# Merged pole powers, a second mixer that ends inside attention, and a new order at the seams, in a two-layer hybrid mixer block

## The chip, the cores and the metric

The kernel runs on one core of one Trainium2 chip. The metric is the device time of one execution, in microseconds, as a median of runs. The engines are named as the profile names them: PE (TensorE, the matmuls; PEld is its weight load), DVE (VectorE), ACT (ScalarE), POOL (GpSimd) and SP (SyncE, which here issues every DMA, in program order, on one queue).

## The reference

Two layers work on 1024 latent tokens and 256 context tokens of width 1024. Each layer modulates and normalises, projects in, runs four mixers of width 256 side by side, gates them, projects out and adds to the residual.

```python
for l in range(DEPTH):                                  # 2
    need_ctx = l < DEPTH - 1
    h_l = rms_norm(x, g_pre[l]) * (1 + sc_l) + sh_l     # the same for ctx
    p_l = h_l @ w_in[l]
    a_l, a_c = mla_mixer(...)                           # attention, low-rank keys
    g_l, g_c = gqa_mixer(...)                           # attention, grouped keys
    s_l, s_c = ssm_mixer(...)                           # state-space scan, both directions
    y_l, y_c = hyena_mixer(...)                         # long convolutions by FFT
    out_l = concatenate([a_l, g_l, s_l, y_l]) @ w_out[l]
    x = x + gt_l * rms_norm(out_l, g_post[l])
    if need_ctx: ...                                    # the context only in the first layer
```

The part of the state-space mixer that moves is its discretisation (a_bar, powers of it, and b_bar, from lam, log_step and b) and its end:

```python
y = y + d_skip * u
z = gelu(y)
z = z * sigmoid(z @ glu_w + glu_b)
return z * silu(p[..., w:])
```

## The kernel before

Activations lie transposed: channels on partitions, tokens along the free dimension, in tiles of up to 512 tokens. A product in full precision is three passes over rounded halves, so that the in-projection, for instance, is a run of PE instructions ipc<-hh,whi, ipc<-hl,whi and ipc<-hh,wlo. Results that another stage needs in another layout go through DRAM: uD and yD (input and output of the scan), hyD (input of the hyena mixer), gP, gV, mK, mV, mQ, mS (keys, values and queries), gD (gates), mixD (the four mixers' outputs, 8 blocks of 128 channels).

A layer runs in this order. First the tables: the filters of the hyena mixer (`filters`, whose step by step tile is ht, and whose PE instructions are hps, brow, sps, fdft), the poles of the scan (`ssm_poles`, small DVE instructions on tiles sp and pw) and the scan's tables (`ssm_tables`, which makes sE, sF and sT on DVE and POOL, transposes sE on PE into etp, and stores all of it). In-projection blocks are woven between by the string SCRIPT. Then four lanes, in the order of the letters in LANES: s the scan (`ssm`), p the preparation of queries, keys and values (`prep`), h the long convolution (`hyena`), f the end of the scan (`ssm_finish`, with `hyena_ctx` for the context in the first layer). LANES is "spfh" in the first layer and "hspf" in the second. The lanes stand under a high priority, and the in-projection of the gates (`inproj_gate`) below it: a list scheduler takes gate matmuls where the lanes' next PE instruction is not ready in its model, so that gate matmuls are filler. What it decides is fixed in the program: each engine runs its instructions in that order, and waits where one is not ready.

The scan goes over groups of channels. For one group PE makes the drive (drv), DVE and POOL turn and scan it (sD, sV), and PE reads it out (sy, three matmuls for each of the group's channel blocks: one with smt and two with sfm). In the kernel before, sy of a group stands right behind that group's scan in the program.

Attention (`attention`) runs units of one pair of heads by 256 queries: 40 in the first layer, 32 in the second. For each it loads keys kst, values vst (once for a pair) and queries aq; makes scores aS and acx; takes row maxima am on DVE and exponentials aP on ACT; transposes apt; splits into aPh (ACT) and aPl (DVE); and makes apo. A generator `side` is pumped once or more in a unit: it makes the gate vectors, loads the output weights (owr) and, in the first layer, the modulation of the second (mraw). A list `later` holds pieces that run at the next pump. `outproj` then reads mixD (omx) and gD (ogt) tile by tile, multiplies them on DVE, splits them on ACT (omh) and POOL (oml), and makes ops on PE.

Of the kernel before, what the change touches and what calls it, by code (L numbers as in the profile page):

```python
# [187 lines left out]
class K:  # L188
# [34 lines left out]
    def mm(self, out, lhsT, rhs, start=True, stop=True):  # L223
        self.keep(self.nc.tensor.matmul(out, lhsT, rhs, start=start, stop=stop))  # L224
# [7 lines left out]
    def tt(self, out, a, b, op, eng=None):  # L232
        self.keep((eng or self.nc.vector).tensor_tensor(out=out, in0=a, in1=b, op=op))  # L233
# [17 lines left out]
    def tr(self, out, in_):  # L251
        p = in_.shape[0]
        self.keep(self.nc.tensor.transpose(out, in_, self.ident[:p, :p]))  # L253
# [52 lines left out]
    def feed(self, P, tag, shape, srcs, ahead):  # L306

        queue, srcs = [], iter(srcs)

        def more():  # L310
            src = next(srcs, None)
            if src is not None:
                t = P.tile(shape, F32, tag=tag, name=tag, bufs=ahead + 1)
                self.load(t, src)
# [8 lines left out]
    def mod_feed(self, P, blocks):  # L323

        return self.feed(P, "mraw", [128, 2, 512],
                         (self.A["w_mod"][l, b, :, k:k + 2] for l, b in blocks for k in range(0, 8, 2)), 2)
# [610 lines left out]
    def ssm_poles(self, l, P, Q):  # L937

        nc, A = self.nc, self.A
        cnt = [0]  # L940

        def t16(n=1):
            cnt[0] += 1
            return P.tile([128, 16] if n == 1 else [128, n, 16], F32, name=f"sp{cnt[0]}", tag=f"sp{cnt[0]}")
# [3 lines left out]
        self.load(lr, A["lam_re"][l])  # L948
        self.load(li, A["lam_im"][l])
        for d in range(2):  # L950
            self.load(ls[d * 64:d * 64 + 64, :], A["log_step"][l, d].partition_broadcast(64))

        def exp_parts(z):
# [11 lines left out]
            Ti = P.tile([128, 16], I32, name=f"spi{cnt[0]}", tag=f"spi{cnt[0]}")  # L965
# [44 lines left out]
        pw = P.tile([128, 2, 9, 16], F32, name="pw")  # L1010
# [8 lines left out]
        inv, qr, qi = t16(), t16(), t16()  # L1019
# [13 lines left out]
        c8 = Q.tile([128, 16], F32, name="c8")  # L1033
        ns8 = Q.tile([128, 16], F32, name="ns8")
        ts(c8, cm8, -1.0, 1.0, MUL, ADD)
        ts(ns8, s8, -1.0)
        rho = self.cp.tile([128, 16], F32, tag="rho", name="rho", bufs=2)
# [6 lines left out]
        def cm_b(o, a, b, n, eng=None):  # L1044

            u, v, w, z = (P.tile([128, 8, 16], F32, tag=f"scm{i}", name="scm")[:, :n] for i in range(4))
            br, bi = (b[i].unsqueeze(1).to_broadcast([128, n, 16]) for i in range(2))
            tt(u, a[0], br, MUL, eng)
            tt(v, a[1], bi, MUL, eng)
            tt(w, a[0], bi, MUL, eng)  # L1050
            tt(z, a[1], br, MUL, eng)
            tt(o[0], u, v, SUB, eng)
# [958 lines left out]
```

## Time and profile before

| | us |
|---|---|
| median of 3 runs | 2169.95 (2166.62 to 2171.66) |
| the profiled execution | 2168.31 |
| its span, first to last instruction | 2166.5 |
| PE busy | 1933.1 (89%) |
| DVE busy | 1557.0 (72%) |
| POOL busy | 972.2 (45%) |
| ACT busy | 896.6 (41%) |

The span is the time from the first to the last instruction, and the profiled execution's own time is 1.8 us more. Matmuls are pipelined and their busy times overlap a little. The stages of the profiled execution, in us from the span's start: start 0 to 72, first layer's tables 72 to 290, scan 295 to 417, preparation and hyena 417 to 712, attention 737 to 1058, output projection 1060 to 1210, second layer's tables to 1420, scan to 1540, the rest of its mixers to 1790, attention to 2054, output projection to the end.

### The profile page before, as it was taken

How to read it: one execution, taken by the hardware profiler on the slowest of the kernel's cores; microseconds unless marked ns; L12 is line 12 of the kernel's file. 1: busy time of each engine (PE TensorE's matmuls, PEld its weight loads, DVE VectorE, ACT ScalarE, POOL GpSimd, SP SyncE). 2: the span in 40 equal slices, each digit the busy share in tenths (PEclk: the TensorE clock that was granted, in tenths of full speed). 3: DMA queues.
4: the chain of work that ended last, by engine and by line, in shares of the span. 5: the costliest groups of instructions: out<-in, count | busy, mean ns of one | idle time of the engine just before them, and what ended most of it. 6: DMA issues, size and time to landing. Idle time of an engine off the chain costs nothing.

```text
span 2166.5 us, 31419 instructions
## 1 busy us (share of the span) xinstructions
PE 1933.1 (89%) x10811; PEld 1602.2 (74%) x10811; DVE 1557.0 (72%) x2969; ACT 896.6 (41%) x1926; POOL 972.2 (45%) x782
## 2 busy tenths in 40 slices
PE   6988998899889599899998898988889979999888
PEld 2677887777768477788777677887766667899766
DVE  5699349757776488788653498479769868999721
ACT  2422234224234367667423222344224227788611
POOL 0757236584461144434156558246566624340034
PEclk9798899899999899999899998999899989999999
DMA  7323365337656545452343423364457675561063
GB/s 254 97 91 136 108 222 142 98 118 239 201 174 197 147 126 154 139 160 80 90 142 123 139 99 130 113 232 137 128 161 223 204 213 142 150 169 46 12 184 126
DMA packets 261280, 316.55 MB, mean 146 GB/s; under 512 B 46671, under 2 KB 203599, under 8 KB 257793
## 3 DMA queue, kind: packets, MB, share of 16 engines
q1 hardware_dynamic: 261120, 314.55, 47.6%
q8 instruction: 85, 1.39, 0.3%
q14 instruction: 75, 0.61, 0.1%
HBM read 207.61 MB, written 106.86 MB: 145 GB/s over the span
## 4 chain that ended last, share of the span: by engine, by line
PE 47%; DVE 29%; DMA 10%; issue 7%; POOL 3%; ACT 2%; SPq 2%; POOLq 0%; DVEq 0%; ACTq 0%
PE ipc L224 9%; PE apo L224 7%; PE apt L253 6%; PE aS L224 6%; PE ops L224 6%; DVE lU L233 3%; DVE sD L233 3%; PE mps L224 2%; SPq L201 2%; DVE sp L233 2%; PE acx L224 2%; PE fdft L224 2%; PE hps L224 1%; DVE lX L233 1%; DVE sV L233 1%
## 5 line engine op out<-in xcount | busy, mean ns | idle before, releaser
L224 PE MATMUL ipc<-hh,whi 128*128 128x512 f32 (+2 forms) x992 | 386.7, 390 | 31.4 <-DVE ipt L236 12.8
L224 PE MATMUL ipc<-hh,wlo 128*128 128x512 f32 (+2 forms) x992 | 381.5, 385 | 3.9 <-POOL wlo L233 3.9
L224 PE MATMUL ipc<-hl,whi 128*128 128x512 f32 (+2 forms) x992 | 382.9, 386 | 0.4 <-POOL hl L233 0.4
L224 PEld LDWEIGHTS ipc<-hh,whi 128*128 128x128 f32 x992 | 196.3, 198 | 65.8 <-DVE ipt L236 15.2
L233 DVE TENSOR_TENSOR aPl<-apt,aPh 128x512 fp32r<-128x512 f32 x328 | 223.8, 683 | 20.7 <-ACT aPh L1672 16.9
L1672 ACT CAST aPh<-apt 128x512 fp32r<-128x512 f32 x328 | 186.5, 590 | 124.2 <-PE apt L253 118.3
L224 PEld LDWEIGHTS ipc<-hh,wlo 128*128 128x128 f32 x992 | 196.5, 198 | 35.2 <-POOL wlo L233 4.6
L224 PEld LDWEIGHTS ipc<-hl,whi 128*128 128x128 f32 x992 | 196.9, 198 | 31.2 <-issue 3.8
L233 POOL TENSOR_TENSOR wlo<-wraw,whi 128x512 fp32r<-128x512 f32 x92 | 139.1, 1516 | 137.1 <-ACT whi L462 103.3
L253 PE MATMUL apt<-ident,aP 128*128 128x128 f32 x1312 | 190.5, 276 | 1.2 <-DVE aPl L233 1.0
L224 PE MATMUL aS<-kst,aq 128*128 128x512 f32 x512 | 152.3, 420 | 26.4 <-DMA aq<-gP 20.8
L1637 DVE TENSOR_REDUCE am<-aS 128x1 f32<-128x1024 f32 x128 | 155.5, 1215 | 21.7 <-PE aS L224 21.6
L246 ACT ACTIVATE aP<-aS,am,rs 128x1024 f32<-128x1024 f32 x128 | 155.5, 1215 | 33.5 <-DVE am L243 32.4
L1700 POOL COPY aLB<-am 128x128 f32<-128x128 f32 x72 | 21.0, 292 | 322.8 <-DVE am L1692 322.8
L253 PEld LDWEIGHTS apt<-ident,aP 128*128 128x128 f32 x1312 | 148.3, 141 | 16.7 <-DVE aPl L233 6.4
L224 PE MATMUL apo<-aPh,vst 128*128 128x256 f32 x656 | 138.3, 308 | 15.3 <-ACT aPh L1672 8.7
L224 PE MATMUL apo<-aPl,vst 128*128 128x256 f32 x656 | 123.5, 286 | 1.6 <-DVE aPl L233 1.3
L224 PEld LDWEIGHTS aS<-kst,aq 128*128 128x128 f32 x512 | 88.2, 192 | 41.7 <-issue 21.2
L224 PEld LDWEIGHTS apo<-aPh,vst 128*128 128x128 f32 x656 | 96.2, 190 | 30.6 <-DVE aob L233 15.8
L224 PE MATMUL ops<-owh,omh 128*128 128x512 f32 x288 | 93.5, 405 | 17.1 <-ACT omh L1785 10.8
L224 PEld LDWEIGHTS apo<-aPl,vst 128*128 128x128 f32 x656 | 100.3, 189 | 8.6 <-DVE aPl L233 3.8
L224 PE MATMUL ops<-owl,omh 128*128 128x512 f32 x288 | 93.3, 404 | 0.0
(369 smaller groups left out, 4382.4 us busy)
## 6 DMA issues: line engine op xcount, KB each, us to landing
wraw<-in_w_col_dram SPq DMA_DIRECT2D x64, 256.0 KB
mraw<-in_w_mod_dram SPq DMA_DIRECT2D x32, 512.0 KB
kst<-mK SPq DMA_DIRECT2D x16, 640.0 KB
omx<-mixD SPq DMA_DIRECT2D x18, 512.0 KB
ogt<-gD SPq DMA_DIRECT2D x18, 512.0 KB
k<-kt SPq DMA_DIRECT2D x16, 512.0 KB
lk<-k SPq DMA_DIRECT2D x8, 1024.0 KB
gD<-ipt SPq DMA_DIRECT2D x32, 256.0 KB
```

Source lines behind the costliest of these rows:

```text
L201: return self.nc.sync.dma_start(out=out, in_=in_)
L224: self.keep(self.nc.tensor.matmul(out, lhsT, rhs, start=start, stop=stop))
L233: self.keep((eng or self.nc.vector).tensor_tensor(out=out, in0=a, in1=b, op=op))
L246: self.keep(self.nc.scalar.activation(out=out, in_=in_, func=func, **k))
L253: self.keep(self.nc.tensor.transpose(out, in_, self.ident[:p, :p]))
L1637: self.keep(nc.vector.tensor_reduce(out=x["m"][:, 2 + qi:3 + qi], in_=x["S"][qi], axis=AX.X, op=ALU.max))
L1672: self.keep(nc.scalar.copy(h, ps))
L1700: self.keep(nc.gpsimd.tensor_copy(x["LB"][:, :, o:o + 64], x["m"][:, 10:12].unsqueeze(2).to_broadcast([128, 2, 64])))
```

## The change

Seven things change.

1. `ssm_poles` runs once, in the first layer, for both layers: the small tiles are 128x32 instead of 128x16, the last copies (pe, pf) are made for each layer, and the second layer's result is stored in DRAM (polD) and loaded there. The products with b (bt, bb) and the loads of b and c go to a new function `ssm_drive`, called at the start of `ssm_tables`.
2. In `ssm_tables` the tile sT is made before the transposition etp, and in the first layer the first transposition of a group is put behind the last DVE instruction on sT by an added dependency (`behind`).
3. In `ssm`, the read-out sy of a group comes one group later, in the middle of the next group's scan, and in the first layer it is put behind a DVE instruction of that scan. There are three buffers for sD and two for smt.
4. LANES is "sphf" in the first layer and "hsp" in the second; the hyena mixer's buffers are freed before the last lane, and the pools of that lane lie on the other side of the memory.
5. In the second layer the end of the scan is no lane any more: `finish_steps` runs it inside attention, through `later`, in four chunks of 256 tokens, both halves of the channels in one instruction where that goes.
6. The first loads of output weights and modulation weights get an issue-order token that attention's loads also have, so they stay behind these.
7. In the second layer's output projection a pool `pad` keeps the output projection's tiles away from the place that attention's tiles held.

```diff
-LANES = "spfh", "hspf"
+LANES = "sphf", "hsp"
@@ ssm_poles
-            return P.tile([128, 16] if n == 1 else [128, n, 16], F32, name=f"sp{cnt[0]}", tag=f"sp{cnt[0]}")
+            return P.tile([128, 2, 16], F32, name=f"sp{cnt[0]}", tag=f"sp{cnt[0]}")
...
+        for l in range(2):
+            c8, ns8, _, _, pe, pf = self.pole_views(res[:, l])
+            pf0 = P.tile([128, 2, 8, 16], F32, tag="pf0", name="pf0")
+            nc.vector.tensor_copy(pe[0:64], pw[0:64, :, 7::-1, l, :])
...
+        self.polD = self.dram.tile([128, self.NPOLE], F32, name="polD")
+        self.store(self.polD, res[:, 1])
+        return res[:, 0]
+    def ssm_drive(self, l, P, qr, qi):
...
@@ dit_kernel
-                poles = k.ssm_poles(l, pt.enter_context(k.pool("polt")), Q)
+                if l == 0:
+                    poles = k.ssm_poles(pt.enter_context(k.pool("polt")), Q)
+                else:
+                    poles = Q.tile([128, k.NPOLE], F32, name="poles")
+                    k.load(poles, k.polD)
@@ ssm_tables
+            last = tt(tab[:, 0], tab[:, 0], w1, SUB)
...
             for ri in range(2):
                 ps = self.b1("etp")
                 for g in range(G):
-                    self.tr(ps[:, g * 128:g * 128 + 128], E[:, ri, g].rearrange("p t h -> p (t h)"))
+                    ins = self.tr(ps[:, g * 128:g * 128 + 128], E[:, ri, g].rearrange("p t h -> p (t h)"))
+                    if l == ri == g == 0:
+                        self.behind(ins, last)
@@ ssm
-            mt = P.tile([128, G, 128], F32, tag="smt", name="smt")
+            mt = P.tile([128, G, 128], F32, tag="smt", name="smt", bufs=2)
-            D = P.tile([128, 2, G, 160], F32, tag="sD", name="sD", bufs=2)
+            D = P.tile([128, 2, G, 160], F32, tag="sD", name="sD", bufs=3)
...
+                ins = self.mm(ps[:, g, :], mt[:, g, :], U[:, gc * G + g, lo:hi], True, False)
+                if l == g == 0 and other is not None:
+                    self.behind(ins, other)
...
-            scan(gc, *d)
+            half = scan(gc, *d)
+            other = next(half)
+            if due:
+                read(*due, other)
             yield
-            read(gc, d[1], *R)
+            for _ in half:
+                pass
             yield
+            due = gc, d[1], *R
@@ dit_kernel, the lane f
-                    with k.pool("ssf") as R:
+                    hr.close()
+                    with k.pool("ssf", side="right") as R:
                         weave(k.ssm_finish(l, R, uD, yD, need))
                         if need:
-                            with k.pool("hyc") as Q:
+                            with k.pool("hyc", side="right") as Q:
                                 weave(k.hyena_ctx(l, Q, hyD, *kf[2:]))
@@ side
                 if cols:
                     yield from k.mod_next(1, steps, M)
+                else:
+                    yield from k.finish_steps(l, M, uD, yD)
+                    for _ in range(5):
+                        yield
@@ finish_steps, for each chunk of 256 tokens, each function at a later pump
+            def skip():
+                for hf in range(2):
+                    self.stt(y[:, hf], g[:, hf], dd[:, hf:hf + 1], y[:, hf], MUL, ADD)
+                self.act(g, y, AF.Square)
+            def inner():
+                self.ts(g, g, 0.044715, 1.0, MUL, ADD)
+                self.tt(g, g, y, MUL)
+                self.act(g, g, AF.Tanh, scale=0.7978845608028654)
+            def gelu():
+                self.stt(g, g, 1.0, y, ADD, MUL)
+            def glu():
+                ps = self.f("sglu").rearrange("p (h n) -> p h n", h=2)
+                for hf in range(2):
+                    for k in range(2):
+                        self.mm(ps[:, hf], gw[:, k, hf * 128:hf * 128 + 128], g[:, k], k == 0, k == 1)
+                    self.act(y[:, hf], ps[:, hf], AF.Tanh, scale=0.25, bias=gb[:, hf:hf + 1])
+            def out():
+                self.stt(y, y, 1.0, g, ADD, MUL)
+                self.store(self.mixD[:, 4:6, c], y)
@@ feed (mod_feed and out_weights give token=self.loads, "ald0" or "ald1")
+                if token and n[0] <= ahead:
+                    self.tc.stamp_issue_order_token(ins.ins, token)
@@ output projection of the second layer
+            hp = ExitStack()
+            hp.enter_context(k.pool("pad")).tile([128, 80 * 256], F32, name="pad")
```

At the seam between the first layer's mixers and its attention, SP's queue of before holds the last mixer stores (mixD from sth and hcz; hcz is the output of the context's hyena) and the first weights of the side work ahead of the loads of keys, values and queries:

```order
L201 DMA mixD_77<-sth 128x256 x4
L201 DMA gD_78<-ipt 128x512
L201 DMA owr<-in_w_out_dram 128x512 x2
L201 DMA gD_78<-ipt 128x256
L201 DMA owr<-in_w_out_dram 128x512 x2
L201 DMA mraw<-in_w_mod_dram 128x1024 x2
L201 DMA mixD_77<-hcz_5082 128x256
L201 DMA mraw<-in_w_mod_dram 128x1024
L201 DMA mixD_77<-hcz_5090 128x256
L201 DMA kst<-gP_4000 64x2560 x2
L201 DMA vst<-gV_4001 128x10x192
L201 DMA aq<-gP_4000 64x2x256 x6
```

Of the kernel after, the same queue around the same loads:

```order
L201 DMA sgy<-yD_81 128x256
L201 DMA sgg<-uD_80 128x256
L201 DMA kst<-gP_4016 64x2560 x2
L201 DMA vst<-gV_4017 128x10x192
L201 DMA aq<-gP_4016 64x2x256 x4
L201 DMA mixD_77<-sth 128x256 x2
L201 DMA gD_78<-ipt 128x512
L201 DMA hck<-k_1313 128x1024
L201 DMA gD_78<-ipt 128x256
L201 DMA sgy<-yD_81 128x256
```

The loads for the first unit now stand ahead of the first of those stores and of the loads (hck, sgy, sgg) for the rest of lane f.

At the seam between the second layer's mixers and its attention, PE of before ends the mixers with sglu (the product with glu_w), between the first scores:

```order
L224 MATMUL ipc<-hl,whi 128x512
L224 MATMUL ipc<-hh,wlo 128x512
L224 MATMUL sglu<-sz,sgw 128x256 x4
L224 MATMUL aS<-kst,aq 128x512 x4
L224 MATMUL sglu<-sz,sgw 128x256 x4
L224 MATMUL acx<-kst,aq 128x256 x4
L224 MATMUL aS<-kst,aq 128x512 x8
```

PE of after makes one of its four sglu groups inside a unit of attention:

```order
L224 MATMUL apo<-aPh,vst 128x256 x4
L224 MATMUL apo<-aPl,vst 128x256 x4
L224 MATMUL acx<-kst,aq 128x256 x4
L224 MATMUL sglu<-sgg,sgw 128x256 x4
L262 MATMUL apt<-ident,aP 128x128 x4
L224 MATMUL apo<-aPh,vst 128x256 x2
```

What stands ahead of the first aS there is a run of 49 ipc.

At the end of the second layer's attention, SP of before stores the last attention outputs (aob) and then loads for the output projection:

```order
L201 DMA aq<-mS_15131 32x2x256 x4
L201 DMA mixD_11567<-aob 128x256 x4
L201 DMA omx<-mixD_11567 128x8x128
L201 DMA ogt<-gD_11568 128x8x128
L201 DMA oxt<-xD 128x1024
```

SP of after:

```order
L201 DMA aq<-mS_14959 32x2x256 x3
L201 DMA mixD_11583<-aob 128x256 x3
L201 DMA omx<-mixD_11583 128x8x128
L201 DMA ogt<-gD_11584 128x8x128
L201 DMA oxt<-xD 128x1024
L201 DMA mixD_11583<-aob 128x256
L201 DMA omx<-mixD_11583 128x8x128
```

The first tile's loads now stand one store earlier.

## Rows read from the trace of the kernel before

**Rows 1.** Mean granted TensorE clock and span, by core.
```profile
core 0: 2166.5 us, clock 0.940
```

**Rows 2.** PE's waits, 0 to 100 us: total, times, longest in us.
```profile
PE xps L253 <- DMA ident<-in_ident_dram: 6.9, 1, 6.9
```

**Rows 3.** DVE's timeline at the start: start, busy us, instruction, idle before.
```profile
33.67 1.29 DVE L233 TENSOR_TENSOR fw<-fw3r 128x512 f32<-128x512 f32 x2 [3.59 <-DMA fw3r<-in_f_w_dram]
```

**Rows 4.** PE's waits, 100 to 290 us.
```profile
PE brow L224 <- DVE ht L233: 10.6, 2, 6.7
PE etp L253 <- DVE sE L233: 4.4, 2, 3.7
```

**Rows 5.** Busy us (instructions) by stretch: length, PE, PEld, DVE, ACT, POOL, clock, DMA, GB/s.
```profile
100.00:200.00 100.00, 82.43 (x477) 70.30 (x476) 97.47 (x227) 24.48 (x46) 64.32 (x46) 0.88 0.24 88
...
300.00:417.00 117.00, 100.48 (x564) 91.77 (x563) 111.40 (x163) 41.18 (x101) 68.53 (x71) 0.91 0.50 157
...
720.80:741.30 20.50, 4.53 (x12) 3.34 (x12) 2.52 (x4) 0.20 (x1) 6.52 (x4) 0.50 0.90 228
...
1250.00:1275.00 25.00, 23.84 (x134) 20.27 (x133) 24.62 (x68) 8.35 (x14) 13.60 (x9) 1.00 0.17 59
...
1900.00:2000.00 100.00, 100.00 (x722) 92.80 (x721) 93.83 (x168) 81.25 (x174) 21.25 (x31) 1.00 0.40 108
```

**Rows 6.** PE's waits, 290 to 420 us.
```profile
PE sy L224 <- POOL wlo L233: 5.9, 2, 4.2
```

**Rows 7.** PE's waits, 420 to 716 us.
```profile
PE ipc L224 <- DVE ipt L236: 9.5, 4, 2.8
```

**Rows 8.** The chain that ended last, 700 to 745 us: start, us, what.
```profile
715.15 7.03 DMA mixD<-hcz
...
723.18 0.50 SPq L201
...
726.86 9.78 DMA aq<-gP
...
736.77 2.05 PE aS L224 x4
```

**Rows 9.** DVE's timeline, second layer's poles: their first and last instructions.
```profile
1233.43 0.17 DVE L233 TENSOR_TENSOR sp<-sp 128x16 f32<-128x16 f32 x1 [2.50 <-DMA sp<-in_lam_re_dram]
...
1256.36 0.48 DVE L233 TENSOR_TENSOR pf<-scm 128x128 f32<-128x128 f32 x2
```

**Rows 10.** PE's waits, 1400 to 1545 us.
```profile
PE sy L224 <- DVE sD L233: 14.8, 8, 5.4
```

**Rows 11.** PE's waits, 1755 to 1800 us.
```profile
PE sglu L224 <- DVE sz L236: 5.2, 1, 5.2
PE sglu L224 <- ACT ipt L246: 4.6, 1, 4.6
```

**Rows 12.** Groups by shape, PE and DVE, 1740 to 1797 us: busy, mean ns, idle before.
```profile
L224 PE MATMUL sglu<-sz,sgw 128*128 128x256 f32 x32 | 11.5, 516 | 9.7 <-DVE sz L236 5.2 <-ACT ipt L246 4.6
...
L233 DVE TENSOR_TENSOR sgg<-sgg,sgy 128x256 f32<-128x256 f32 x8 | 3.3, 423 | 0.2
```

**Rows 13.** PE's timeline around 1764 us.
```profile
1763.70 1.24 PE L224 MATMUL sglu<-sz,sgw 128*128 128x256 f32 x5
...
1765.01 0.39 PE L224 MATMUL ipc<-hh,whi 128*128 128x512 f32 x1
1765.24 0.39 PE L224 MATMUL ipc<-hl,whi 128*128 128x512 f32 x1
```

**Rows 14.** DVE's timeline at the end of the second layer's attention.
```profile
2055.33 0.42 DVE L233 TENSOR_TENSOR aob<-aob,alb 128x256 f32<-128x256 f32 x1
2062.89 1.36 DVE L236 SCALAR_TENSOR_TENSOR omx<-omx,ogt 128x512 f32<-128x512 f32 x3 [7.13 <-DMA ogt<-gD]
```

**Rows 15.** PE's timeline at the same place.
```profile
2054.21 0.38 PE L253 MATMUL alb<-ident,aLB 128*128 128x128 f32 x2
2065.38 1.22 PE L224 MATMUL ops<-owh,omh 128*128 128x512 f32 x2 [10.79 <-ACT omh L1785]
```

More of the change, by code (lines that the diff above doesn't have):

```diff
@@ L252, in tr @@
         p = in_.shape[0]
-        self.keep(self.nc.tensor.transpose(out, in_, self.ident[:p, :p]))
+        ins = self.nc.tensor.transpose(out, in_, self.ident[:p, :p])
+        self.keep(ins)
+        return ins
     def setup(self, es):
@@ L304, in mod_block, with feed @@
         return ms
-    def feed(self, P, tag, shape, srcs, ahead):
-        queue, srcs = [], iter(srcs)
+    def feed(self, P, tag, shape, srcs, ahead, token=None):
+        queue, srcs, n = [], iter(srcs), [0]
         def more():
@@ L1018, in ssm_poles @@
         tt(mr, e1, mr, SUB)
-        inv, qr, qi = t16(), t16(), t16()
+        inv = t16()
+        c8, ns8, qr, qi = (res[:, :, i * 16:i * 16 + 16] for i in range(4))
         tt(inv, lr, lr, MUL)
@@ L1042, in ssm_poles, with cm_b @@
         nc.vector.memset(pw[:, 1, 0], 0.0)
[L1044 to L1052, printed above, removed]
-            tt(o[1], w, z, ADD, eng)
+        def cm_b(o, a, b, sh):
+            m = "p (a b c) -> p a b c" if len(sh) == 3 else "p (a b) -> p a b"
+            k = dict(zip("abc", sh))
+            u, v, w, z = (P.tile([128, 128], F32, tag=f"scm{i}", name="scm")[:, :math.prod(sh)].rearrange(m, **k)
+                          for i in range(4))
+            br, bi = (b[i].unsqueeze(1).to_broadcast([128, *sh]) for i in range(2))
+            tt(u, a[0], br, MUL)
+            tt(v, a[1], bi, MUL)
+            tt(w, a[0], bi, MUL)
+            tt(z, a[1], br, MUL)
+            tt(o[0], u, v, SUB)
+            tt(o[1], w, z, ADD)
         u, v, w = t16(), t16(), t16()
@@ L1168, in ssm_tables @@
             yield
+            tab = P.tile([128, 2, G, 16, 10], F32, tag="sT", name="sT")
+            sh = [128, G, 16, 10]
+            ar, ai = (big[:, i, gs].unsqueeze(3).to_broadcast(sh) for i in range(2))
+            br, bi = (small[:, i, gs].unsqueeze(2).to_broadcast(sh) for i in range(2))
+            w1 = P.tile(sh, F32, tag="sw0", name="sr0")
+            w2 = P.tile(sh, F32, tag="sw1", name="sr1")
+            tt(tab[:, 0], ar, br, MUL)
+            tt(w1, ai, bi, MUL)
+            last = tt(tab[:, 0], tab[:, 0], w1, SUB)
+            tt(tab[:, 1], ar, bi, MUL, pool)
+            tt(w2, ai, br, MUL, pool)
+            tt(tab[:, 1], tab[:, 1], w2, ADD, pool)
+            self.store(tD[:, :, gs], tab.rearrange("p r g a b -> p r g (a b)"))
             et = P.tile([128, 2, G, 128], F32, tag="sET", name="sET")
@@ L1543, in attention @@
         token = self.token = f"att{l}"
+        self.loads = f"ald{l}"
         self.later = []
@@ L1988, in dit_kernel @@
                         xns = []
+        if not need:
+            hp.close()
 _OUTS = [((1, 1024, 1024), "float32")]
```

123 lines of the change are left out of this document (73 added, 50 removed).

## The prediction

> **What bounds the kernel now.** PE is busy for 1933 of 2166.5 us, so the question is where PE waits and what its clock was there. I read the granted clock first: its mean is 0.940 [rows 1]. It has two levels, 1.2 and 2.4 GHz, so 0.06 x 2166.5 / 0.5 = 260 us of the span ran at the lower one. A wait of PE is therefore paid twice: in the window by stretch, the 20.5 us from 720.8 us on, most of it the large wait, stand at 0.50 [rows 5]. Then PE's waits, stage by stage. The large ones are at four places: at the first layer's seam into attention one of 20.8 us, for a load of queries [rows 8]; at the end of the second layer's attention 10.79 us [rows 15]; at the end of its scan lane 5.2 and 4.6 us for sglu [rows 11]; and in its scan eight of together 14.8 us for sD [rows 10]. Last, the busy shares by stretch: the first layer's tables and scan belong to DVE (97.47 of 100 us, 111.40 of 117), and the second layer's attention to PE, with DVE close behind (100.00 and 93.83 of 100) [rows 5].
>
> **The change part by part**, made against the profiled 2168.31 us; the median lies 1.64 us above that and is brought in at the end. What stands where in after is from the order of instructions.
>
> 1. *Start, -2 (from -4 to +2).* PE's transposes wait 6.9 us for ident [rows 2]. ident moves up five places on SP, since the four loads of b and c leave the places ahead of it: a gain of up to half of that wait. Against it, four more small loads stand ahead of the first weight load; at the 0.50 us that an issue took elsewhere [rows 8] that is +2 for PE's first matmul. The wider pole instructions and the second layer's copies are hidden: DVE stands idle for 3.59 us in one piece a little later, waiting for a load [rows 3].
>
> 2. *First layer's tables and scan, 0 (from -8 to +8).* Waits of PE for brow, etp and sy (10.6, 4.4 and 5.9 us) [rows 4, 6] look like the prize, but they come from DVE being full. The edits move PE's instructions, not DVE's: neither the transpositions put behind sT nor the read-outs one group later take anything off DVE. The two stretches could be shorter by DVE's idle time alone, 2.5 and 5.6 us [rows 5], hence -8. The other end: bt and bb move into the tables, six instructions at 0.42 us (the nearest shape) [rows 12], 2.5 us, plus one more wait like that of 5.9 us [rows 6]. What `behind` holds up on PE is all that is queued there: filler, drv for later groups, hyena's matmuls. I take the middle.
>
> 3. *First layer's preparation and hyena, +4 (from 0 to +17).* In after more filler and hyena work stands ahead of the last read-out, so less is left here. Between the first and the fifth prt (one in each token chunk of the preparation) PE has 465 rows, not 542. A 512-wide matmul follows the last by 0.23 us [rows 13]; 77 of them are 17.7 us. If the chain through DVE, POOL and DRAM sets the pace of the chunks, all of it turns into waits; there are such waits already, 9.5 us in four for ipt [rows 7]. But other matmuls come later and fill elsewhere; I take a quarter.
>
> 4. *First layer's seam, -20 (from -23 to -10).* In before the chain reads: a store of hcz that took 7.03 us, then the issue of kst at 723.18, the load of aq, 9.78 us to landing, and aS at 736.77 [rows 8]. In after the loads for the first unit stand ahead of these stores, on buffers that lane f no longer holds, and 34 ipc stand between the last hco and aS. The gap of 20.8 goes, and with it half of the 4.53 us that PE was busy at the lower clock [rows 5]: -23. If the loads are issued early but wait for something else, one load's 9.78 us or so stays: about -10. What is late next is the first unit's own chain.
>
> 5. *Second layer's tables, -6 (from -10 to 0).* The poles run from 1233.43 to 1256.84 on DVE, mixed with the filters' instructions [rows 9], and behind them DVE is full (24.62 of 25 us) [rows 5]. The instructions that go make perhaps 10 of these 23.4 us; PE gains what of it ended in waits and in lower clock, and I take somewhat more than half. Zero, if PE's filler hides DVE there.
>
> 6. *Second layer's scan, -7 (from -15 to +3).* Read-outs one group later face a DVE that is a group ahead; the 14.8 us [rows 10] could go whole. Half stays in the estimate, because filler taken here lacks later.
>
> 7. *Second layer's preparation, +3 (from 0 to +8)*, by the same reasoning as 3, with half its bound.
>
> 8. *Second layer's scan end, -15 (from -17 to -6).* Out of the seam go 9.7 us of waits ahead of sglu and 11.5 us in which its 32 matmuls ran [rows 12]. Into attention go 32 at 0.25 us (1.24 us for five) [rows 13], 8 us, at full cost since PE is at 100 of 100 there [rows 5]: 9.7 + 11.5 - 8 = 13.2, and some 2 for the scores that ran between at the lower clock. DVE: five instructions for each of eight pieces at 0.42 us [rows 12] are 17 us; with both halves merged I estimate 14. They fall into about ten units of 8.2 us (264 us for 32 units), where DVE has 6.2% of 82 us, 5 us, free [rows 5], and PE's 8 us more give it 8: 1 us is left over, which the rounding holds. If they do not overlap so well, 9 us come back: -6.
>
> 9. *Second layer's seam, +6 (from 0 to +13).* With sglu gone, 49 ipc (11.3 us at 0.23 [rows 13]) are all that PE has between the last key projection (mkn) and aS. Behind mkn come a copy, the stores of the keys, and in SP's queue a gD store between the halves of kst, which waits for a gate block that ends some 24 ipc, 5.6 us, before PE runs dry; then vst and aq. With a landing time like 9.78 us [rows 8] PE waits 4 us, and about 2 for the clock. Zero if landing is quick; +13 if it starts only as PE goes dry.
>
> 10. *Second layer's end, -5.5 (from -7 to -3).* DVE ends aob at 2055.75, then waits 7.13 us for ogt, and ops starts at 2065.38 [rows 14, 15]. In after the first tile's loads stand ahead of the last store, but two gt multiplies (0.7 us each, from 0.42 for half the width [rows 12]) stand between aob and omx. 1.4 + 1.36 + 1.13 (the end of omx to ops) from 2055.75 on gives 2059.6, 5.7 earlier.
>
> Sum: -2 + 0 + 4 - 20 - 6 - 7 + 3 - 15 + 6 - 5.5 = -42.5, so 2125.8 for such a profiled run, and with 1.64 a median of 2127.5.
>
> **The rivals.**
>
> *Filler spent early* (2152). Gates are the only filler, and moving it forward only moves the waits: 3 at +17, 7 at +8, 6 at 0, so -42.5 + 13 + 5 + 7 = -17.5. For it: the stages before are DVE's [rows 5]. Against: the waits that are there now are small pieces [rows 7].
>
> *The seams do not close* (2144.5). The loads stand early in the order but wait for buffers or land late; the change then does not do what it says. 4 at -10, 9 at +13: -25.5. For it: landing times of 7 to 10 us [rows 8].
>
> *Waits behind DVE grow into a loop, slower* (2183.5). In the first layer's scan PE stands in order behind a DVE instruction of the next group, and drv, which DVE needs, stands behind that. If each of eight read-outs then costs the longest wait of the second layer's scan, 5.4 us [rows 10], and 2.3 us for the clock as in 4, that is 62 us; less the 5.9 that are there [rows 6], +56, hence +13.5 in all. It decides against the change from 42.5 us of new waits on, 5.3 for each group. Against it: the third buffer of sD lets drv run ahead.
>
> *Everything in DVE's stages is gained* (2108.5): 3 at 0, 4 at -23, 5 at -10, 6 at -15, together 19 more.
>
> *The clock costs little* (2132). The rows give 260 us at the lower level, so up to 130 us lost in busy stretches [rows 1]. The Trainium skill, page "TensorE: Matmul & The Clock Gate", section "What's actually happening", says that the ramp penalty is under 1% of a typical kernel's span. By that it would be some 22 us here, a sixth, and of the 5.8 us for the clock in 4 and 8 (2.3 and 3.5) only 1 would be gained: 4.8 less. This trace, with a mean of 0.940, speaks against it.
>
> **How the numbers follow.** Chances: forecast 0.48, filler spent early 0.20, seams not closed 0.12, everything gained 0.08, loop 0.07, cheap clock 0.05. The likeliest gives 2127.5. The ten terms' ends lie some 3, 8, 9, 6, 5, 9, 4, 5, 6 and 2 us off; as they are independent, together (root of the sum of squares) 19. With the rivals above it, the range is 2102 to 2158: the loop, half of the early filler's upper part and the best of the gains are left out. About 0.2%, 4.3 us, is what a measurement can tell from no change: faster by more 0.88, within it 0.05 (early filler at its worst), slower 0.07 (the loop).
>
> **What would show it.** Step 4: aS within 2 us of the ipc before it, and no long stretch at 0.50 there. Step 8: no sglu ahead of the second layer's aS, attention longer by 8 to 9 us and DVE near 97%. Step 9: a wait of some 4 us of aS for aq or kst. Step 10: a gap near 5 us ahead of ops. Steps 2 and 3: brow and sy still wait for DVE, and the last sy of the first layer comes no earlier than now. The prediction is wrong if the first layer's scan gets longer by over 20 us, if aS waits at either seam for over 10 us, or if DVE sets the pace of attention.

## The result, and the profile after

The changed kernel takes 2146.85 us (median of four runs, 2136.19 to 2148.95) against 2168.28 (2165.57 to 2171.66): a ratio of 0.9896, 95% interval 0.9875 to 0.9918. That is 21.4 us, where the forecast was 42.5; it lies in the range. The profiled run of after took 2148.95 us, the longest of the four.

The span and mean granted clock of after; before it was 0.940 [rows 1]:

```profile
core 0: 2147.2 us, clock 0.944
```

Stage by stage, first the kernel before. Columns: stretch, its length, then busy us (instructions) of PE, PEld, DVE, ACT, POOL, granted clock, DMA share, GB/s. The stretches are: start and first layer's tables; its scan; the rest up to its first aS; the second layer's tables; its scan; its preparation and hyena; the seam; its attention.

```profile
0.00:279.00 279.00, 238.26 (x1209) 176.50 (x1209) 190.87 (x519) 78.78 (x156) 128.80 (x102) 0.88 0.42 139
279.00:417.30 138.30, 119.33 (x669) 107.99 (x669) 113.12 (x166) 46.38 (x114) 71.85 (x74) 0.93 0.51 157
417.30:736.80 319.50, 276.02 (x1491) 231.60 (x1490) 200.78 (x339) 98.67 (x226) 154.46 (x106) 0.95 0.61 183
...
1205.50:1416.60 211.10, 193.93 (x1045) 163.54 (x1044) 143.41 (x404) 57.77 (x114) 108.53 (x77) 0.90 0.37 124
1416.60:1541.20 124.60, 104.58 (x604) 95.42 (x603) 118.97 (x180) 45.41 (x111) 70.46 (x56) 0.89 0.49 161
1541.20:1751.00 209.80, 184.64 (x901) 143.65 (x899) 165.03 (x222) 66.52 (x149) 138.27 (x96) 0.96 0.63 190
1751.00:1797.00 46.00, 34.47 (x152) 27.38 (x152) 25.64 (x58) 17.86 (x42) 5.73 (x4) 0.85 0.78 216
1797.00:2054.40 257.40, 254.58 (x1786) 225.78 (x1784) 236.63 (x430) 203.11 (x434) 60.15 (x77) 1.00 0.38 102
```

The same stages of after:

```profile
0.00:262.60 262.60, 231.99 (x1163) 171.42 (x1164) 191.55 (x529) 75.27 (x143) 130.82 (x100) 0.88 0.43 143
262.60:448.20 185.60, 152.53 (x853) 138.21 (x853) 142.01 (x195) 57.51 (x139) 98.43 (x94) 0.89 0.42 132
448.20:723.40 275.20, 255.76 (x1353) 211.75 (x1352) 175.02 (x308) 93.98 (x213) 120.46 (x84) 0.97 0.67 197
...
1190.70:1386.90 196.20, 171.91 (x945) 143.88 (x944) 126.09 (x282) 55.97 (x109) 105.80 (x76) 0.91 0.40 132
1386.90:1494.50 107.60, 87.15 (x521) 79.29 (x521) 101.13 (x164) 41.08 (x103) 54.98 (x47) 0.92 0.50 162
1494.50:1730.30 235.80, 216.11 (x1110) 177.82 (x1109) 170.87 (x241) 73.93 (x161) 150.10 (x106) 0.96 0.57 175
1730.30:1754.00 23.70, 12.25 (x51) 9.68 (x51) 2.92 (x6) 2.08 (x5) 0.00 (x0) 0.84 0.93 243
1754.00:2040.10 286.10, 272.35 (x1855) 239.70 (x1854) 257.36 (x463) 217.94 (x463) 66.07 (x80) 0.98 0.42 118
```

Such rows are read by length minus PE's busy time, which is PE's idle time. The stages end at the same marks (the last brow, the last sy, the first aS, the first drv), but filler moved across them, so a shorter stage is a gain only as far as PE's work in it did not shrink. The two last rows are not cut alike: in before the attention row starts 19.1 us behind the first aS (1777.9), in after 0.9 us behind it (1753.1). From the first aS to the last apo it is 276.5 us in before, with PE idle for 9.6, and 287.0 in after, with 13.8.

Up to the first aS the first layer needs 723.4 us instead of 736.8, 13.4 less; PE's idle time there falls by 20.1 (103.2 to 83.1) while its busy time rises by 6.7 for as many instructions. Its attention and output projection add 1.4 us to the gain (last ops at 1190.7, not 1205.5). In the second layer the tables are 14.9 us shorter with 22.0 us less of PE's work in them, and the scan 17.0 us shorter with 17.4 less: no idle time is gained in either. From the last ops of the first layer to the last apo, after takes 849.4 us and before 848.9. That is a sum of two changes, which the rows of the whole stretch show (before, then after): PE's busy time falls by 12.4 us and its idle time rises by 12.9.

```profile
1205.50:2054.40 848.90, 772.20 (x4480) 655.77 (x4478) 689.67 (x1292) 390.66 (x848) 383.15 (x309) 0.94 0.48 144
1190.70:2040.10 849.40, 759.77 (x4476) 650.37 (x4474) 658.38 (x1154) 391.00 (x840) 376.95 (x309) 0.95 0.48 146
```

The end gives 5.3, up to the first ops.

Waits of PE in after, first layer, four stretches (start, tables, scan, seam): total us, times, longest.

```profile
PE xps L262 <- DVE sp L245: 3.3, 1, 3.3
...
PE brow L224 <- DVE ht L235: 5.0, 1, 5.0
PE etp L262 <- DVE sT L235: 4.3, 1, 4.3
...
PE lout L224 <- DVE lX L235: 14.3, 3, 7.2
...
PE sy L224 <- DVE sV L235: 5.4, 2, 3.4
...
PE aS L224 <- ACT aP L255: 2.2, 1, 2.2
```

The wait of 20.8 us at the seam [rows 8] is gone, brow waits half as long as in [rows 4], and a new wait for hyena's lX stands in the scan. In the second layer:

```profile
PE hps L224 <- ACT fh L255: 10.9, 1, 10.9
...
PE sy L224 <- DVE sD L235: 13.0, 5, 6.7
...
PE aS L224 <- DMA aq<-gP: 11.5, 1, 11.5
```

sy still waits nearly as in [rows 10], hps waits 10.9 us for a filter step (1.8 in before), and the seam has a wait of its own. The chain there: the last store of keys, the issue of kst behind it, the load of queries, the first scores.

```profile
1733.94 4.46 DMA mK<-sp
1738.56 0.49 SPq L201
...
1743.45 9.43 DMA aq<-gP
...
1753.12 2.05 PE aS L224 x4
```

Two kst of 640 KB and a vst of 960 KB are issued ahead of aq. At the 243 GB/s of that stretch these 2.2 MB take some 9 us, an estimate from these sizes and that row; so the 9.43 us of aq can be the transfer of what stands ahead of it. No run tried fewer bytes there.

At the end of the second layer's attention DVE now goes from aob by gt to omx without a wait for a load [rows 14], and PE's wait is 3.1 us, not 10.79 [rows 15] (two gps stand between):

```profile
2041.09 0.42 DVE L235 TENSOR_TENSOR aob<-aob,alb 128x256 f32<-128x256 f32 x1
2041.43 0.69 DVE L235 TENSOR_TENSOR gt<-gps,gt 128x512 f32<-128x512 f32 x1
2042.72 0.69 DVE L235 TENSOR_TENSOR gt<-gps,gt 128x512 f32<-128x512 f32 x1 [0.60 <-PE gps L224]
2043.33 1.35 DVE L245 SCALAR_TENSOR_TENSOR omx<-omx,ogt 128x512 f32<-128x512 f32 x3
```

```profile
PE ops L224 <- ACT omh L1884: 3.1, 1, 3.1
```

### The profile page after: what moved, and what is told of

It reads as the page before. It is cut to its first block, busy times and chain, and to the rows that moved or that the text cites. A ratio compares the mean times of both kernels' runs of the same rounds, so it can differ in the third digit from the quotient of the medians.

```text
span 2147.2 us, 31272 instructions
## 1 busy us (share of the span) xinstructions
PE 1927.6 (90%) x10811; PEld 1601.8 (75%) x10811; DVE 1531.3 (71%) x2843; ACT 900.5 (42%) x1918; POOL 967.6 (45%) x782
## 4 chain that ended last, share of the span: by engine, by line
PE 47%; DVE 25%; DMA 10%; issue 7%; POOL 5%; SPq 3%; ACT 3%; POOLq 0%; DVEq 0%; ACTq 0%
PE ipc L224 12%; PE apo L224 6%; PE aS L224 5%; PE apt L262 5%; PE ops L224 5%; SPq L201 3%; DVE sD L235 3%; DVE lU L235 2%; PE mps L224 2%; PE acx L224 2%; DVE sp L235 1%; PE hps L224 1%; PE fdft L224 1%; DVE sV L235 1%; DVE lX L235 1%
## 5 line engine op out<-in xcount | busy, mean ns | idle before, releaser
L224 PE MATMUL aS<-kst,aq 128*128 128x512 f32 x512 | 153.7, 423 | 17.9 <-DMA aq<-gP 11.5
L255 ACT ACTIVATE aP<-aS,am,rs 128x1024 f32<-128x1024 f32 x128 | 155.7, 1216 | 21.2 <-PE aS L224 15.2
L1799 POOL COPY aLB<-am 128x128 f32<-128x128 f32 x72 | 21.2, 294 | 309.6 <-DVE am L1791 307.8
```

The source lines that it names most:

```text
L224: ins = self.nc.tensor.matmul(out, lhsT, rhs, start=start, stop=stop)
L255: self.keep(self.nc.scalar.activation(out=out, in_=in_, func=func, **k))
L1799: self.keep(nc.gpsimd.tensor_copy(x["LB"][:, :, o:o + 64], x["m"][:, 10:12].unsqueeze(2).to_broadcast([128, 2, 64])))
```

## The experiments

All are compared with the kernel before by ratio (95% interval in brackets); the changed kernel is 0.9896 [0.9875, 0.9918]. A 0.001 is 2.2 us. Single executions of one kernel of this family lie up to 20 us apart (2154.88 to 2175.37 in the second run of 2), so differences of 3 us between medians are not read. A single trace scatters too: in after and the ten runs below that keep its order of PE instructions up to the first aS, that aS stands at 717.2 to 727.4 us, with PE busy for 637.7 to 643.9 us ahead of it.

**1. The added dependencies taken out of the first layer.**

```diff
-                    if l == ri == g == 0:
-                        self.behind(ins, last)
-                if l == g == 0 and other is not None:
-                    self.behind(ins, other)
```

> The changed kernel without the added dependencies (behind) of the first layer's transpositions and read-outs. Theory: both stretches belong to DVE, so the place of PE's instructions in them is worth nothing: 2147 us, within 4 us. Rival one: the dependencies gain, and without them it is over 2152 us. Rival two: they hold PE back, and without them it is below 2142 us.

Measured: 2162.03 us, 0.9982 [0.997, 0.9994]. The dependencies are worth 15 us by the medians and 19 by the ratios; rival one holds, and my theory falls. How, the stages up to the first aS show (cut at the same marks as above):

```profile
0.00:278.20 278.20, 241.80 (x1169) 181.32 (x1169) 191.73 (x529) 77.20 (x153) 128.75 (x100) 0.85 0.41 139
278.20:415.60 137.40, 115.54 (x626) 102.53 (x626) 110.73 (x163) 45.26 (x111) 70.64 (x74) 0.91 0.50 155
415.60:732.20 316.60, 291.69 (x1575) 246.73 (x1574) 208.42 (x340) 103.45 (x231) 151.02 (x104) 0.96 0.59 178
```

PE's idle time is 83.2 us, against 83.1 in after, but the first aS comes at 732.2, not 723.4, and outside the scatter of the eleven traces. The difference is in PE's busy time, 649.0 against 640.3 us for the same instructions, again outside that scatter, and in the clock: weighted by length, what is missing to 1.00 makes 134 us at the lower level, against 120 in after (each sum of (1 - clock) x length / 0.5). By the clock records of the two traces PE was busy in 117.9 and in 100.8 us of that time. In before an ipc follows the last by 0.43 us at the lower level (from 75.9 us on) and by 0.23 at the upper [rows 13], so nearly half of the difference, an estimate of 8 us, is what the clock cost: most of the 8.7. The rest of the 15 us comes later, with another order in the second layer, whose seam waits 16.9 us for aq in this run. Both dependencies went at once, and PE's order around them is another one too; which of these makes the clock lower was not tried.

**2. The second layer's poles computed there again.** First by the merged function, for both layers; then by the old one, for one layer.

```diff
-                    poles = Q.tile([128, k.NPOLE], F32, name="poles")
-                    k.load(poles, k.polD)
+                    poles = k.ssm_poles(pt.enter_context(k.pool("polt")), Q, 1)      # the first run
+                    poles = k.ssm_poles_own(l, pt.enter_context(k.pool("polt")), Q)  # the second: 128x16
```

> The changed kernel with the second layer's poles computed in the second layer again (with the instructions on 128x32, for both layers, as in the first), nothing stored or loaded for them. Theory from the traces: the second layer's tables lasted as long per PE work as before, a wait of 10.9 us of hps for fh having taken the place of others, so that taking the poles out was worth at most 4 us: 2147 to 2151 us. Rival, the prediction's term 5: 6 to 10 us come back, 2153 to 2157 us.

Measured: 2174.5 us, 1.0045 [1.0029, 1.0061]: 28 us more than after by the medians, which neither side had.

> The changed kernel with the second layer's poles computed in the second layer by the old instructions on 128x16 (the first layer's merged ones stay, their second half unused). The run that computed both layers' poles there again was 28 us slower than the changed kernel, where I had expected at most 10. Theory: DVE's small instructions delay everything behind them in the second layer's tables, whose pace DVE sets, so that their 10 us of work cost more than 15 us: 2162 to 2172 us. Rival: the surplus came from doing both layers there; with one layer's alone it is 2150 to 2157 us, as the prediction's term 5 has it.

Measured: 2162.1 us, 0.9979 [0.9962, 0.9996]: 15 us more than after by the medians and 18 by the ratios, at the lower edge of the theory's band and outside the rival's. The poles' removal from the second layer was worth 15 us, not 6. In this run DVE has 264.8 us of work in the second layer's tables and scan, against 227.2 in after; the two last 334.6 us instead of 303.8, with 28.7 more of PE's busy time. Most of that is work that stands elsewhere in after (118 more PE instructions); the whole stretch from the last ops of the first layer to the last apo has the same work:

```profile
1186.20:2047.30 861.10, 770.78 (x4475) 657.71 (x4474) 696.11 (x1274) 390.42 (x840) 381.05 (x309) 0.94 0.47 144
```

PE is idle there for 90.3 us, against 89.6 in after, and busy for 770.8, against 759.8. In the first run, with PE's 10811 instructions as in after, 21.2 of the 23.7 us by which its span is longer (2170.9, not 2147.2) are PE's busy time (1948.8, not 1927.6), at a mean clock of 0.930, not 0.944. So the poles' time on DVE does come out as PE's time, but as the same work at a lower clock, more than as waits.

**3. In the second layer sT behind the transposition again.**

```diff
-            tab = P.tile([128, 2, G, 16, 10], F32, tag="sT", name="sT")
+            if l == 0:
+                last = rotation()        # the tile sT, its six instructions and its store
...
+            if l == 1:
+                rotation()               # behind kfp, as before the change
```

> The changed kernel, but in the second layer the tile sT is made behind the transposition again, as before; the first layer stays as changed. Theory: the new wait of hps for fh in the second layer's tables (10.9 us) comes from sT, sr and sF standing ahead of the filter's fq and fa on DVE; with sT later it falls below 3 us and the time is about 2139 us. Rival: DVE is full there either way, so that the wait moves to brow, etp or hps elsewhere, and the time stays at 2147 us.

Measured: 2145.98 us, 0.9906 [0.9891, 0.9921], as after. The rival holds: the wait of hps stays,

```profile
PE hps L224 <- ACT fh L255: 9.3, 1, 9.3
```

so it does not come from sT standing ahead. DVE has little idle time in the stretch ahead of that wait's end in either kernel (busy for 21.57 of 24 us in after, for 21.60 of 24 here); what would have to move to let the filter step through was not found.

**4. The first layer's seam alone, in the kernel before.**

```diff
-LANES = "spfh", "hspf"
+LANES = "sphf", "hspf"
...
+                    hr.close()
-                    with k.pool("ssf") as R:
+                    with k.pool("ssf", side="right") as R:
-                            with k.pool("hyc") as Q:
+                            with k.pool("hyc", side="right") as Q:
```

> The kernel before with one part of the change alone: in the first layer the hyena mixer ahead of the scan's end and the context's hyena, that lane's pools on the other side of the memory, the hyena's buffers freed earlier (the pools in the second layer too). Theory, the prediction's term 4: the wait of 20.8 us of aS falls below 3 us, and the time to 2146 to 2150 us. Rival: what PE saves at the seam it waits for in the stages before, as the changed kernel's first layer, with the seam closed, came only 13 us earlier to aS: 2158 us or more.

Measured: 2169.54 us, 1.0016 [1.0006, 1.0026]. The time is the rival's. The first layer's gain is there: first aS at 724.8, last ops at 1192.3, 13.2 us earlier than before. It lasts to the second layer's first aS (1763.6, not 1777.9) and is given back behind that. The stretch up to the first aS, the second layer's attention, and PE's waits between 1750 and 1790 us:

```profile
0.00:724.80 724.80, 640.68 (x3365) 521.48 (x3365) 503.12 (x1022) 224.89 (x496) 346.20 (x278) 0.92 0.51 160
1763.60:2052.80 289.20, 274.57 (x1852) 239.85 (x1852) 257.23 (x470) 217.21 (x465) 65.91 (x80) 0.97 0.38 110
```

```profile
PE sglu L224 <- DVE sz L236: 9.2, 3, 3.4
PE aS L224 <- DMA sgy<-yD: 8.7, 1, 8.7
```

Up to the first aS PE's idle time falls by 19.1 us (103.2 to 84.1), nearly the wait of 20.8, but its busy time rises by 7.1 (633.6 to 640.7): the mean clock is 0.92 in either kernel, so the time at the lower level did not go with the wait (some 118 and 116 us). By the clock records PE is busy in 104.7 us of it, where it was in 88.9 in before. The edit puts the second layer's last lane on the other side of the memory as well, and there aS comes earlier but sglu's waits now lie behind it, inside attention. No run has the edit for the first layer alone.

**5. The second layer's scan end as a lane again.**

```diff
-LANES = "sphf", "hsp"
+LANES = "sphf", "hspf"
...
-                else:
-                    yield from k.finish_steps(l, M, uD, yD)
-                    for _ in range(5):
-                        yield
```

> The changed kernel with the second layer's scan end as a lane again, ahead of attention (lanes hyena, scan, preparation, end), nothing of it inside attention. Theory from the two traces: moving it gained little, since attention took it up with 11 us more of waits and 8 us of matmuls, and aS waits 11.5 us at the seam: undone, some 10 us of waits for sglu come back, the wait of 11.5 goes, attention gets shorter by about 19 us, and the time is 2147 to 2152 us. Rival, the prediction's terms 8 and 9 (-15 and +6): undone, the time is about 2156 us.

Measured: 2148.76 us, 0.9919 [0.9902, 0.9935]: 2 us more than after by the medians and 5 by the ratios, in the theory's band. With the interval of after's ratio the difference can be anything from 1 us less to 11 more, so the prediction's 9 is not excluded. With the lane, these waits stand at the seam:

```profile
PE aS L224 <- DMA sgy<-yD: 9.6, 1, 9.6
PE sglu L224 <- DVE sz L245: 8.8, 3, 3.4
```

Without it, aS waits 11.5 us instead of 9.6, and from there to the last apo PE is idle for 13.8 us, instead of 15.5 with the lane: 25.3 and 25.1 us together. What the lane cost came back at these two places.

**6. More work behind the last key projection.**

```diff
-LANES = "sphf", "hsp"
+LANES = "sphf", "sph"
```

> The changed kernel with the lanes of the second layer in the order scan, preparation, hyena, so that hyena matmuls and gate blocks stand behind the last key projection. In the changed kernel aS waits 11.45 us for aq at the second layer's seam. Theory: the keys' loads start only when the last store of keys is done (4.5 us) and land 9 us after issue, and 49 gate matmuls are too little cover; with more PE work behind the last key projection the wait falls below 5 us and the time to about 2140 us (before 2168, changed kernel 2147). Rival: the cover is only moved, and as much comes back as waits for the scan or the hyena steps: 2147 us, with aS waiting less and lout or sy waiting more.

Measured: 2139.53 us, 0.988 [0.9866, 0.9894]. The median is the theory's, though the wait fell less than it said, and the intervals of the ratio overlap with after's:

```profile
PE aS L224 <- DMA aq<-gP: 7.3, 1, 7.3
```

**7. The preparation's tiles elsewhere**, so that kst need not wait for what lies in its place.

```diff
-                    with k.pool("pre") as Q:
+                    with k.pool("pre", side="right" if l else "left") as Q:
```

> The changed kernel with the preparation's tiles of the second layer on the other side of the memory, away from the place where attention's first key tile will lie. Theory: kst is issued only when the last mK store has read its tile (4.5 us after the store's issue), since the two share memory; apart, the loads start about 4.5 us earlier, aS's wait of 11.5 us falls to about 7, and the time is about 2141 us. Rival: the loads wait for the stores to gP to land or for the gate blocks in the queue, and the wait stays at 10 to 12 us and the time at 2147 us.

Measured: 2145.22 us, 0.9898 [0.9884, 0.9911]: the rival. The issue of kst still follows the end of the last mK store:

```profile
1730.63 4.50 DMA mK<-sp
...
1735.27 0.50 SPq L201
```

So shared memory with the preparation's tiles is not, or not alone, what holds it; which of the waits on that load does stays open.

**8. Where attention's idle time comes from.** In after ACT stands for sglu and for DVE, and PE's largest waits behind its first aS are for DVE (first ACT's two rows, then PE's):

```profile
ACT sgy L255 <- PE sglu L224: 11.4, 8, 1.9
ACT sgg L255 <- DVE sgg L235: 4.3, 2, 2.4
...
PE apo L224 <- DVE aob L235: 4.0, 6, 2.2
PE alb L262 <- DVE aPl L235: 3.0, 2, 2.1
```

Four runs tried causes. The tanh on sglu's result at a later pump:

```diff
-                    self.act(y[:, hf], ps[:, hf], AF.Tanh, scale=0.25, bias=gb[:, hf:hf + 1])
-                self.later.append(out)
+                self.later.append(lambda: gate(ps))     # gate: the two tanh, then out a pump later
-                    for _ in range(5):
+                    for _ in range(6):
```

> The changed kernel with the two tanh on sglu's result one pump later than the matmuls that make it. In the changed kernel ACT stands eight times, 11.4 us in all, in its queue in front of these tanh and waits for sglu, with casts to aPh queued behind; PE is idle for 13.75 us in the second layer's attention, against 2.8 before. Theory: this order on ACT makes most of the idle time; with the tanh later PE's idle time there falls to about 6 us and the time to about 2140. Rival, from the prediction: VectorE is what is full there, so the idle time stays above 11 us and the time at 2147 us.

Measured: 2153.35 us, 0.9943 [0.9927, 0.9958], 6.5 us slower than after by the medians; neither side had that. A wait that after hardly has appeared:

```profile
PE apt L262 <- DVE aPl L235: 11.5, 10, 1.9
```

apt and sglu share two PSUM buffers, and sglu's result now holds one for a whole unit. That led to the next theory, that it is this buffer in after too:

```diff
-                ps = self.f("sglu").rearrange("p (h n) -> p h n", h=2)
+                ps = self.b2("sglu")[:, :512].rearrange("p (h n) -> p h n", h=2)
```

> The changed kernel with the result of sglu in attention in one of the two PSUM buffers of the scores instead of one of the two that the transpositions apt use. Theory, formed after the run with the tanh later (6 us slower, PE waiting 11.5 us for aPl ahead of apt): while sglu's result waits for its tanh, apt has one buffer instead of two, and that makes most of PE's 13.75 us of idle time in the second layer's attention; with the buffer elsewhere the idle time falls below 7 us and the time to about 2139 us. Rival: VectorE's 14 us of added work make it, wherever the result lies: idle time above 11 us and 2147 us.

Measured: 2144.37 us, 0.989 [0.9869, 0.9911], as after, and so is the stage from the first aS to the last apo; the theory falls, since PE's idle time is 13.7 us in it:

```profile
1739.00:2025.70 286.70, 272.99 (x1856) 240.49 (x1856) 257.25 (x463) 217.82 (x463) 65.96 (x80) 0.98 0.42 119
```

With this and the order of lanes of run 6 together:

> The changed kernel with both edits that the traces point to: sglu's result in the scores' PSUM buffers, and the lanes of the second layer in the order scan, preparation, hyena. If both act on different waits (idle time in attention; aq at the seam), they add up: about 2133 us. If either only moves a wait, it is about 2140 us, as with the order of lanes alone.

Measured: 2139.34 us, 0.987 [0.9851, 0.989]: the gain of the lanes alone. And on top of that, the tanh one cast later within the unit:

```diff
-                self.later.append(out)
+                self.mid.append(lambda: gate(ps))       # run in the next unit behind its first cast aPh
...
-    ORDER = ("T0 Vh4-1 MC+1 H0 Vl4-1 ...
+    ORDER = ("T0 Vh4-1 MC+1 H0 Y Vl4-1 ...
```

> The kernel with both edits (sglu's result in the scores' PSUM buffers, second layer's lanes scan, preparation, hyena), and in attention the two tanh on sglu's result one cast (aPh) later on ACT, still before that buffer is needed. Where the result lies made no difference (idle time of PE in the second layer's attention as before). Theory: ACT stands in its queue in front of these tanh until PE has made sglu (11.4 us in eight waits in the changed kernel), and the casts behind come late; now ACT's waits for sglu fall below 2 us, PE's idle time there from 13.75 to below 8 us, and the time to about 2134 us. Rival: VectorE's added work, or ACT's waits for VectorE's pieces (6.2 us), make it: PE's idle time stays above 11 us and the time at about 2139 us.

Measured: 2138.62 us, 0.9873 [0.9848, 0.9899]: the rival. ACT no longer waits for sglu there, but more for DVE, and PE is idle for 15.6 us (17.1 in the run before, cut alike):

```profile
ACT sgg L255 <- DVE sgg L235: 9.2, 4, 2.4
```

```profile
1739.00:2029.00 290.00, 274.43 (x1856) 242.60 (x1856) 258.38 (x463) 217.42 (x463) 65.80 (x80) 0.98 0.41 118
```

Neither the buffer nor ACT's queue in front of the tanh is the cause. What is left is DVE's added work, as the rivals had it, or the order in which one pump puts pieces of three chunks on DVE; these two were not told apart.

The kernels with the lanes scan, preparation, hyena in the second layer (2138.6 to 2139.5 us) are the fastest that ran: some 28 us below the kernel before by the medians, and below the changed one by about 7 by the medians and 3 to 6 by the ratios, whose intervals overlap with its own.

## Why the prediction was half right

The direction and the range hold, and so do most of the places; the size is half. The range was 56 us wide, and the measured median lies nearer to the figures of two rivals (2144.5 and 2152) than to the forecast, so that it lies inside says little for the sum. By its steps, in the first layer 14.8 us came of 18, in the second up to the end of attention -0.5 of 19, at the end 5.3 of 5.5. That the first layer came near is luck in part: step 4 fell short, and the added dependencies brought what step 2 denied them.

- *Step 1* is right in its sum: xps waits 3.3 us, not 6.9 [rows 2], and runs 2.4 us earlier. The wait that is left is for DVE's sp, the pole instructions, which the step took as hidden.
- *Step 2* failed in its reason, not in its sum. It said that the place of PE's instructions in a stage that DVE fills is worth nothing. Run 1 shows that the order with the dependencies is worth 9 us by the first aS, at equal idle time, through the clock. I had counted the clock only beside the large waits.
- *Step 3* came out the other way, 22.7 us of idle time ahead of the seam's wait falling to 19.4. The chunks do not run dry. The waits went to the scan instead, where lout for 14.3 us stands.
- *Step 4* is right in its mechanism and too large. The wait went whole, but aS came 12.0 us earlier with this edit alone (run 4), not 20, and 13.4 in after. The step, like the sentence that a wait is paid twice, took the clock as a gain of 2.3 us on top of the wait. Run 4 shows the opposite sign: 19.1 us less of idle time, 7.1 more of busy time.
- *Step 5* was mis-sized: 15 us (run 2), not 6. I priced the time of DVE's instructions and somewhat more than half of it for PE; what came is 11.0 us less of PE's busy time in the second layer at equal idle time.
- *Step 6* failed. sy waits 13.0 us, not 14.8, and the later read-out brought nothing there. Whether the added dependency, which the second layer does not have, would have changed that was not tried.
- *Step 7* came out the other way, as step 3 did: PE's idle time in that stage fell from 25.2 to 19.7 us. The wait of hps of 10.9 us in the tables stands in no step.
- *Steps 8 and 9* together were -9 and measured -2 by the medians and -5 by the ratios (run 5), with -9 inside the interval. Step 9 is the mis-sized one at the seam: 11.5 us of wait, where I had 4. In the trace kst is issued only after the last mK store has ended, 4.46 us, which the sum did not hold; the landing of 9.43 us was as taken [rows 8]. In step 8 the idle time of attention is the miss: 13.75 us, where before has 2.8 from 1797 us on, so 11 more and not the 1 left over from adding up busy times. It is near the step's upper end, which I had for DVE.
- *Step 10* is right to 0.2 us, gt and omx with the very durations.

Of the prediction's own signs of being wrong one came: aS waits over 10 us at a seam, 11.5 at the second. The first layer's scan, from the first drv to the last sy, grew from 121.8 to 137.2 us, less than the 20 that it named, though its last sy comes 30.9 us later.

The rival of seams that do not close described the second layer, and its 2144.5 us is the figure nearest to the measured one; at the first seam it was wrong. The loop did not come: added waits behind DVE were a gain. Two orders with the same idle time differ by 8.7 us of busy time at different clocks (run 1). That is 0.4% of the span but 40% of the whole gain, and leaving it out of the sum was the mistake. The rival of a cheap clock falls: at a mean clock of 0.944 some 240 us of after's 2147.2 are at the lower level, PE is busy in 187 of them by the trace's clock records, and nearly half of these (run 1), an estimate of 90 us, is what the lower level cost. By the page "TensorE: Matmul & The Clock Gate" of the Trainium skill (section "What's actually happening") the ramp costs under 1% of a typical kernel's span. The 90 us are some 4% of this one's, so this trace does not agree with the page.

The parts do not add up to the whole gain of 21 us. Taken back out of the changed kernel, the dependencies cost 15 us and the poles 15 by the medians, which is more than 21 already; the first seam alone, put into the kernel before, gave 12 us at its place and nothing at the end (run 4). Either other parts of the change cost time, or the terms were not independent, as the prediction took them; run 4 speaks for the second, since one edit set the order anew up to the end of the kernel.

## What to carry to other kernels

Where one engine's filler is short, count a closed gap as a gain only once the next place that needs cover is priced: here the second layer's seam and attention took back most of what its last lane gave. A stage that another engine fills can still be worth reordering on the waiting engine, where the granted clock varies: compare busy times for the same instructions, not idle times alone. Work moved into a stage where PE, DVE and ACT are 99, 92 and 79% busy, as before's attention, should be priced by a run, since busy times that add up below 100% did not show the 14 us of idle time that its waits made.

## What the runs showed of the hardware that I had not expected

Two kernels with the same instructions up to the first aS and the same idle time of PE (83.2 and 83.1 us) needed 732.2 and 723.4 us: PE's busy time was 649.0 and 640.3 us, at granted clocks of 0.85, 0.91 and 0.96 against 0.88, 0.89 and 0.97 in the three stages. Closing a wait of 20.8 us, most of it at a clock of 0.50, left the mean clock up to the first aS at 0.92 (run 4). And one order of PE's instructions, executed eleven times, reached the first aS at 717.2 to 727.4 us, with 637.7 to 643.9 us of busy time: a scatter as large as many of the differences that the runs were made for.
